# Row maxima that skip NaN: two row pieces for each load, and a separate tile for the 16-bit keys

## The chip, the core and the metric

The kernel runs on one core of a Trainium2 chip. Its engines work in parallel, each through its own queue in order: ScalarE (ACT in the profile), GpSimd (POOL), VectorE (DVE) and SyncE (SP), which here only issues DMA transfers. They wait for each other by semaphores. TensorE (PE) does nothing in this kernel. The on-chip memory has 128 partitions, and a tile is a stretch of bytes in each of them. The metric is the device time of one launch in microseconds (us), the median of several runs.

## What is computed

```python
batch, seq, dim = 32, 2048, 2048
x = np.random.randn(batch, seq, dim).astype(np.float32)
mask = np.random.rand(batch, seq, dim) < 0.1
x[mask] = np.nan
...
np.nanmax(x, axis=-1).astype(np.float32)
```

That is 65,536 rows of 2048 float32 numbers, 537 MB read, and for each row the largest number that is not NaN (a row of NaN alone gives NaN). The output has 65,536 numbers.

## The kernel before

Each partition takes 512 rows. They are cut into groups (`GROUPS`, line 11): twelve groups of 40 rows a partition, each loaded as five tiles `xt` of 8 rows (64 KB a partition, 8.4 MB in all), then a group of 24 rows in tiles of 7, 6, 5, 4 and 2 rows, and one of 8 rows in tiles of 2, 2, 1, 1, 1 and 1: 71 tiles. The pool of `xt` (line 58) has three buffers, so three tiles can be in flight.

Each tile passes four steps, each of which takes the whole tile:

1. SP loads `xt` (line 74). The load waits until VectorE has done with the tile that held the buffer, three tiles ahead.
2. ScalarE (line 77) reads the upper 16 bits of every number as a signed integer, `[:, 1::2]`, so every second 16-bit word, and writes a 16-bit key over them. The activation function (Prelu with a bias and a scale of -1) maps a number's upper half v to 0x7F7F - v; a positive NaN's upper half, 0x7FC0, falls on the function's other slope and gets the key 0x7F7F + 129.
3. GpSimd (line 85) reads the key in the same place and writes 0x7F7F - key over it. Ordinary numbers get their upper half back; NaN gets -129, which makes the number -255 x 2^120, below all the data.
4. VectorE (line 93) takes the maximum of each row of `xt` as float32 into `acc`.

After a group, VectorE makes `none` from `acc` (line 101: which rows hold only NaN) and `fin` from `acc` and `none` (line 110: turns those rows back to NaN). ScalarE's queue issues the store of `fin` (line 113); it stands there ahead of the ScalarE steps of the tiles that follow.

What sets the order is the order in which the code is written, queue by queue, and the buffers of the pools.

Of the kernel before, what the change touches and what calls it, by code (L numbers as in the profile page):

```python
# [1 line left out]

# [4 lines left out]

GROUPS = [(40, [8] * 5)] * 12 + [
    (24, [7, 6, 5, 4, 2]),
    (8, [2, 2, 1, 1, 1, 1]),
]

TOP = 0x7F7F
NAN = 0x7FC0
LOW = -129  # L20

EDGE = TOP + 0.25

NONE = -255.0 * 2.0**120


@with_exitstack
def kernel(
    ctx: ExitStack,
    tc: tile.TileContext,  # L30
    x: bass.AP,
    axis: bass.AP,
    out: bass.AP,
):

    nc = tc.nc
    P = nc.NUM_PARTITIONS
    f32, i32 = mybir.dt.float32, mybir.dt.int32
    i16, u16 = mybir.dt.int16, mybir.dt.uint16
    ALU = mybir.AluOpType

    nd = len(x.shape)
    assert axis in (-1, nd - 1), axis  # L50
    D = x.shape[-1]

    xr = x.bitcast(i32).flatten_outer_dims()
    R = xr.shape[0]
    of = out.bitcast(i32).flatten_outer_dims().rearrange("r c -> (r c)")
    assert R == P * sum(s for s, _ in GROUPS)

    io = ctx.enter_context(tc.tile_pool(name="io", bufs=3))
    res = ctx.enter_context(tc.tile_pool(name="res", bufs=3))
    sing = ctx.enter_context(tc.tile_pool(name="sing", bufs=1))  # L60
    top = sing.tile([P, 1], f32)
    nc.vector.memset(top, EDGE)  # L62

    r0 = 0
    for s, cuts in GROUPS:
        assert sum(cuts) == s
        xg = xr[r0 : r0 + P * s].rearrange("(p s) d -> p s d", p=P)
        og = of[r0 : r0 + P * s].rearrange("(p s) -> p s", p=P)
        r0 += P * s
        acc = res.tile([P, s], f32, tag="acc")  # L70
        at = 0
        for c in cuts:
            xt = io.tile([P, c * D], i32, tag="xt")
            nc.sync.dma_start(
                out=xt, in_=xg[:, at : at + c].rearrange("p c d -> p (c d)")
            )
            nc.scalar.activation(  # L77
                out=xt.bitcast(u16)[:, 1::2],
                in_=xt.bitcast(i16)[:, 1::2],
                func=mybir.ActivationFunctionType.Prelu,  # L80
                bias=top,
                scale=-1.0,
                alpha=float(TOP - LOW) / (EDGE - NAN),
            )
            nc.gpsimd.tensor_scalar(  # L85
                out=xt.bitcast(i16)[:, 1::2],
                in0=xt.bitcast(u16)[:, 1::2],
                scalar1=-1.0,
                scalar2=float(TOP),
                op0=ALU.mult,  # L90
                op1=ALU.add,
            )
            nc.vector.tensor_reduce(  # L93
                out=acc[:, at : at + c],
                in_=xt.bitcast(f32).rearrange("p (c d) -> p c d", c=c),
                axis=mybir.AxisListType.X,
                op=ALU.max,
            )
            at += c
        none = res.tile([P, s], i32, tag="none")  # L100
        nc.vector.tensor_scalar(  # L101
            out=none,
            in0=acc,
            scalar1=NONE,
            scalar2=float(0x00C00000),
            op0=ALU.is_equal,
            op1=ALU.mult,
        )
        fin = res.tile([P, s], i32, tag="fin")
        nc.vector.tensor_tensor(  # L110
            out=fin, in0=acc.bitcast(i32), in1=none, op=ALU.bitwise_or
        )
        nc.scalar.dma_start(out=og, in_=fin)  # L113


# [1 line left out]
_INS = ['x', 'axis']  # L117
_OUTS = [((32, 2048), 'float32')]

_NUMBERS = {'axis': -1}  # L120


# [26 lines left out]
```

## Time and profile before

| | |
|---|---|
| median of 3 runs | 1747.19 us (1747.01 to 1747.41) |
| the profiled execution | 1748.27 us |
| its span, from the first instruction to the last | 1746.5 us |
| VectorE, ScalarE, GpSimd busy | 1143, 1182, 1175 us |
| read from memory, mean rate over the span | 536.87 MB, 308 GB/s |

The profile shows one execution. Busy time counts an engine's instructions; the idle time before an instruction is put down to what released it last. In a row of the timeline stand the start, the length, the engine, the line of the kernel, the operation, its tiles and shapes, the count of merged instructions and the idle time before with its releaser. In a row of the groups stand the line, the engine, the operation, the shapes and the count, then the busy time and the mean length in ns, then the idle time before. In a row of the DMA issues stands the time from issue to landing at the end. The busy share of ScalarE, GpSimd and the DMA engines in 40 slices of the span, in tenths, shows a pattern of peaks and gaps throughout:

```profile
ACT  4865956856857757758668668567577586586553
POOL 0959577587586585595595595595595595595854
DMA  9595976966967867868768669669569669569343
```

### The profile page before, as it was taken

Reading aid. Unit: us, or ns where it says so; the run is one execution under the profiler, and the core shown is the slowest. Engines: PE = TensorE matmul, PEld = TensorE weight load, DVE = VectorE, ACT = ScalarE, POOL = GpSimd, SP = SyncE. Lnnn points to the kernel's source line nnn. Section 1 sums busy time; section 2 is a strip of 40 time slices with the busy share of each in tenths; the row PEclk is TensorE's granted clock in tenths of the full one; section 3 lists DMA queues with packets and bytes.
Section 4 is the critical chain, followed back from the end, with each engine's and each line's share of the span. In section 5 each row is a group of like instructions: output and inputs, shape, how many; then the busy total and the mean of one; then the engine's idle time right before and its main releaser. Section 6 shows DMA issues by size and latency. Waiting matters only on the chain.

```text
span 1746.5 us, 655 instructions
## 1 busy us (share of the span) xinstructions
DVE 1143.4 (65%) x100; ACT 1182.0 (68%) x72; POOL 1174.7 (67%) x75
## 2 busy tenths in 40 slices
DVE  0568585585585585675674774864865856856886
ACT  4865956856857757758668668567577586586553
POOL 0959577587586585595595595595595595595854
DMA  9595976966967867868768669669569669569343
GB/s 420 234 444 246 385 308 269 385 282 294 385 264 312 361 263 338 334 268 360 313 264 384 293 260 408 265 263 429 241 267 410 265 264 428 245 264 411 142 192 144
DMA packets 12244, 537.17 MB, mean 308 GB/s; under 512 B 3152, under 2 KB 3152, under 8 KB 3152
## 3 DMA queue, kind: packets, MB, share of 16 engines
q1 hardware_dynamic: 10224, 536.88, 72.6%
q10 hardware_dynamic: 2016, 0.26, 0.1%
q14 instruction: 4, 0.03, 0.0%
HBM read 536.87 MB, written 0.26 MB: 308 GB/s over the span
## 4 chain that ended last, share of the span: by engine, by line
DVE 26%; POOL 26%; ACT 22%; DMA 19%; issue 6%; ACTq 0%; POOLq 0%; DVEq 0%
POOL xt L85 26%; DVE acc L93 24%; ACT xt L77 22%; DMA xt<-in_x_dram 19%; DVE none L101 2%; ACTq L113 0%; POOLq L144 0%; DVE fin L110 0%; ACTq L77 0%; POOLq L85 0%; DVEq L93 0%
## 5 line engine op out<-in xcount | busy, mean ns | idle before, releaser
L85 POOL TENSOR_SCALAR xt<-xt 128x16384 int16<-128x16384 uint16 (+4 forms) x71 | 1174.5, 16542 | 566.4 <-ACT xt L77 565.6
L77 ACT ACTIVATE xt<-xt,top 128x16384 uint16<-128x16384 int16 (+4 forms) x71 | 1180.7, 16642 | 533.8 <-DMA xt<-in_x_dram 323.1
L93 DVE TENSOR_REDUCE acc<-xt 128x8 f32<-128x16384 f32 (+4 forms) x71 | 1102.6, 15535 | 598.9 <-POOL xt L85 598.9
L101 DVE TENSOR_SCALAR none<-acc 128x40 int32<-128x40 f32 (+2 forms) x14 | 39.1, 2790 | 0.5
L77 ACT ACT_TABLE_LOAD x1 | 1.3, 1283 | 23.0 <-DMA xt<-in_x_dram 23.0
L110 DVE TENSOR_TENSOR fin<-acc,none 128x40 int32<-128x40 int32 (+2 forms) x14 | 2.8, 197 | 0.5
L62 DVE MEMSET top<- 128x1 f32 x1 | 0.1, 59 | 0.8 <-PEq L130 0.8
L130 POOL MEMSET const-float32-0.0<- 128x1 f32 x1 | 0.1, 98 | 0.2 <-issue 0.2
L130 POOL MEMSET const-bfloat16-1.0<- 128x1 bf16 x1 | 0.1, 102 | 0.0
L130 POOL MEMSET const-uint8-127<- 128x1 uint8 x1 | 0.1, 102 | 0.0
L130 POOL MEMSET const-float32-1.0<- 128x1 f32 x1 | 0.1, 98 | 0.0
## 6 DMA issues: line engine op xcount, KB each, us to landing
xt<-in_x_dram SPq DMA_DIRECT2D x1, 7168.0 KB, 19.6
xt<-in_x_dram SPq DMA_DIRECT2D x1, 6144.0 KB, 16.9
xt<-in_x_dram SPq DMA_DIRECT2D x3, 2048.0 KB, 7.3
xt<-in_x_dram SPq DMA_DIRECT2D x1, 5120.0 KB, 14.6
xt<-in_x_dram SPq DMA_DIRECT2D x1, 4096.0 KB, 12.0
xt<-in_x_dram SPq DMA_DIRECT2D x4, 1024.0 KB, 4.7
xt<-in_x_dram SPq DMA_DIRECT2D x60, 22.0
out_dram<-fin ACTq DMA_DIRECT2D x12, 20.0 KB, 19.6
```

The costliest lines, as they stand in the source:

```text
L62: nc.vector.memset(top, EDGE)
L77: nc.scalar.activation(out=xt.bitcast(u16)[:, 1::2], in_=xt.bitcast(i16)[:, 1::2], func=mybir.ActivationFunctionType.Prelu, bias=top, scal ...
L85: nc.gpsimd.tensor_scalar(out=xt.bitcast(i16)[:, 1::2], in0=xt.bitcast(u16)[:, 1::2], scalar1=-1.0, scalar2=float(TOP), op0=ALU.mult, op1= ...
L93: nc.vector.tensor_reduce(out=acc[:, at : at + c], in_=xt.bitcast(f32).rearrange("p (c d) -> p c d", c=c), axis=mybir.AxisListType.X, op=A ...
L101: nc.vector.tensor_scalar(out=none, in0=acc, scalar1=NONE, scalar2=float(0x00C00000), op0=ALU.is_equal, op1=ALU.mult,)
L110: nc.vector.tensor_tensor(out=fin, in0=acc.bitcast(i32), in1=none, op=ALU.bitwise_or)
L130: nc = _bacc.Bacc("TRN2", target_bir_lowering=False, num_devices=1)
```

## The change

- The groups become eleven of 42 rows, one of 28, one of 14 and one of 8. Seventy full tiles have 7 rows (56 KB a partition, `WIDE`), loaded at once; the last 22 rows come in loads of 4 rows down to 1, with up to five loads to a tile.
- ScalarE, GpSimd and VectorE go over a tile in pieces: 4 rows and then 3 in a full tile, 1 to 4 in the last ones. A piece has its own ScalarE, GpSimd and VectorE instruction.
- ScalarE writes the keys of a piece packed into a tile of their own, `kt`, from a new pool `mid` with two buffers of 4 rows (16 KB each). GpSimd reads them there, side by side, and writes the result into every second word of `xt`, as before.
- The store of `fin` goes to SP's queue, behind the first load of the group after the next one; the last two come at the end.
- A small activation on `top` at the start brings the table load of ScalarE ahead of the first load's landing.

```diff
-GROUPS = [(40, [8] * 5)] * 12 + [
-    (24, [7, 6, 5, 4, 2]),
-    (8, [2, 2, 1, 1, 1, 1]),
+FULL = [[4, 3]]
+GROUPS = [[FULL] * 6] * 11 + [
+    [FULL] * 4,
+    [[[4], [3]], [[3], [2], [2]]],
+    [[[2], [1, 1], [1], [1], [1]], [[1]]],
 ]
+WIDE = 7
+PIECE = 4
...
     io = ctx.enter_context(tc.tile_pool(name="io", bufs=3))
+    mid = ctx.enter_context(tc.tile_pool(name="mid", bufs=2))
...
+    warm = sing.tile([P, 1], f32)
+    nc.scalar.activation(out=warm, in_=top, func=PRELU, alpha=0.5)
...
-        for c in cuts:
-            xt = io.tile([P, c * D], i32, tag="xt")
-            nc.sync.dma_start(
-                out=xt, in_=xg[:, at : at + c].rearrange("p c d -> p (c d)")
-            )
-            nc.scalar.activation(
-                out=xt.bitcast(u16)[:, 1::2],
-                in_=xt.bitcast(i16)[:, 1::2],
...
-            nc.gpsimd.tensor_scalar(
-                out=xt.bitcast(i16)[:, 1::2],
-                in0=xt.bitcast(u16)[:, 1::2],
...
+        for tl in g:
+            xt = io.tile([P, WIDE * D], i32, tag="xt")
+            base = at
+            for ld in tl:
+                c = sum(ld)
+                nc.sync.dma_start(
+                    out=xt[:, (at - base) * D : (at - base + c) * D],
+                    in_=xg[:, at * D : (at + c) * D],
+                )
+                if len(stores) > 1:
+                    nc.sync.dma_start(**stores.pop(0))
+                for c in ld:
+                    xp = xt[:, (at - base) * D : (at - base + c) * D]
+                    kt = mid.tile([P, PIECE * D], u16, tag="kt")
+                    nc.scalar.activation(
+                        out=kt[:, : c * D],
+                        in_=xp.bitcast(i16)[:, 1::2],
...
+                    nc.gpsimd.tensor_scalar(
+                        out=xp.bitcast(i16)[:, 1::2],
+                        in0=kt[:, : c * D],
...
+                    nc.vector.tensor_reduce(
+                        out=acc[:, at : at + c],
+                        in_=xp.bitcast(f32).rearrange("p (c d) -> p c d", c=c),
...
-        nc.scalar.dma_start(out=og, in_=fin)
+        stores.append(dict(out=og, in_=fin))
+    for st in stores:
+        nc.sync.dma_start(**st)
```

What stands in the queues, at two places. ScalarE's queue around the end of the first group, before the change (numbered names are the buffers; in brackets what the instruction waits for: DMAHW is a load, Pool is GpSimd):

```order
L77 ACTIVATE xt_82<-xt_82,top_64 128x16384 [waits DMAHW3_49,DVE_49]
L77 ACTIVATE xt_87<-xt_87,top_64 128x16384 [waits DMAHW4_49,DVE_49]
L77 ACTIVATE xt_98<-xt_98,top_64 128x16384 [waits DMAHW5_49,DVE_49]
L113 DMA out_0_dram<-fin_94 128x40 [waits DVE_49]
L77 ACTIVATE xt_103<-xt_103,top_64 128x16384 [waits DMAHW6_49,Pool_49]
```

And ScalarE's queue from its first piece on, after the change:

```order
L96 ACTIVATE kt_74<-xt_72,top_67 128x8192 [waits DMAHW0_49]
L96 ACTIVATE kt_78<-xt_72,top_67 128x6144
L96 ACTIVATE kt_84<-xt_82,top_67 128x8192 [waits DMAHW1_49,Pool_49]
L96 ACTIVATE kt_88<-xt_82,top_67 128x6144 [waits Pool_49]
L96 ACTIVATE kt_94<-xt_92,top_67 128x8192 [waits DMAHW2_49,Pool_49]
```

The store with its wait for VectorE has left this queue; from the third piece on each piece waits for GpSimd, which has to have read the key buffer's last piece.

SP's queue near the end, after the change (`xt_854` is the second tile of the 14-row group, `xt_875` the first of the 8-row group, `fin_839` belongs to the 28-row group):

```order
L87 DMA xt_854<-in_x_dram 128x6144 [waits DMAHW6_49,DVE_49]
L87 DMA xt_854<-in_x_dram 128x4096 [waits DMAHW4_49]
L87 DMA xt_854<-in_x_dram 128x4096
L87 DMA xt_875<-in_x_dram 128x4096 [waits DMAHW7_49,DVE_49]
L92 DMA out_0_dram<-fin_839 128x28 [waits DVE_49]
L87 DMA xt_875<-in_x_dram 128x4096 [waits DMAHW0_49]
L87 DMA xt_875<-in_x_dram 128x2048 [waits DMAHW1_49]
```

The store of the 28-row group stands among the loads of the last tiles and waits for VectorE; the stores ahead of it in this queue (two groups late) have no such wait listed.

More of the change, by code (lines that the diff above doesn't have):

```diff
@@ L47 @@
     ALU = mybir.AluOpType
+    PRELU = mybir.ActivationFunctionType.Prelu
     nd = len(x.shape)
@@ L55 @@
     of = out.bitcast(i32).flatten_outer_dims().rearrange("r c -> (r c)")
-    assert R == P * sum(s for s, _ in GROUPS)
+    rows = [sum(sum(sum(ld) for ld in tl) for tl in g) for g in GROUPS]
+    assert R == P * sum(rows)
     io = ctx.enter_context(tc.tile_pool(name="io", bufs=3))
+    mid = ctx.enter_context(tc.tile_pool(name="mid", bufs=2))
     res = ctx.enter_context(tc.tile_pool(name="res", bufs=3))
@@ L62 @@
     nc.vector.memset(top, EDGE)
+    warm = sing.tile([P, 1], f32)
+    nc.scalar.activation(out=warm, in_=top, func=PRELU, alpha=0.5)
+    stores = []
     r0 = 0
-    for s, cuts in GROUPS:
-        assert sum(cuts) == s
-        xg = xr[r0 : r0 + P * s].rearrange("(p s) d -> p s d", p=P)
+    for s, g in zip(rows, GROUPS):
+        xg = xr[r0 : r0 + P * s].rearrange("(p s) d -> p (s d)", p=P)
         og = of[r0 : r0 + P * s].rearrange("(p s) -> p s", p=P)
@@ L71 @@
         at = 0
-        for c in cuts:
-            xt = io.tile([P, c * D], i32, tag="xt")
-            nc.sync.dma_start(
-                out=xt, in_=xg[:, at : at + c].rearrange("p c d -> p (c d)")
-            )
-            nc.scalar.activation(
-                out=xt.bitcast(u16)[:, 1::2],
-                in_=xt.bitcast(i16)[:, 1::2],
[L80 to L85, printed above, removed]
-                out=xt.bitcast(i16)[:, 1::2],
-                in0=xt.bitcast(u16)[:, 1::2],
[L88 to L99, printed above, removed]
+        for tl in g:
[15 more added lines that the diff above has]
+                        in_=xp.bitcast(i16)[:, 1::2],
+                        func=PRELU,
+                        bias=top,
+                        scale=-1.0,
+                        alpha=float(TOP - LOW) / (EDGE - NAN),
+                    )
+                    nc.gpsimd.tensor_scalar(
+                        out=xp.bitcast(i16)[:, 1::2],
+                        in0=kt[:, : c * D],
+                        scalar1=-1.0,
+                        scalar2=float(TOP),
+                        op0=ALU.mult,
+                        op1=ALU.add,
+                    )
+                    nc.vector.tensor_reduce(
+                        out=acc[:, at : at + c],
+                        in_=xp.bitcast(f32).rearrange("p (c d) -> p c d", c=c),
+                        axis=mybir.AxisListType.X,
+                        op=ALU.max,
+                    )
+                    at += c
```

## The prediction

> **What bounds the kernel now.** I read the page's first part first, to see whether an engine is full, and then the DMA queue.
>
> ```profile
> DVE 1143.4 (65%) x100; ACT 1182.0 (68%) x72; POOL 1174.7 (67%) x75
> q1 hardware_dynamic: 10224, 536.88, 72.6%
> SPq L74 <- DVE acc L93: 1676.5, 67, 55.4
> ```
>
> No engine is full and the loads take 73% of the DMA time. The third line, from the list of what the load queue waited for, names the reason: of 1746.5 us, SP stood 1676.5 us until a VectorE maximum released a buffer. So the bound is the loop load, ScalarE, GpSimd, VectorE, next load through three buffers. The chain of work that ended last (start, length, what) shows its first load and one turn:
>
> ```profile
> 0.74 22.16 DMA xt<-in_x_dram
> ...
> 386.36 18.44 ACT xt L77
> 404.86 18.29 POOL xt L85
> 423.18 17.23 DVE acc L93
> 440.44 2.07 DVE none L101
> 442.53 0.21 DVE fin L110
> 442.76 0.34 ACTq L113
> 443.20 18.43 ACT xt L77
> 461.71 18.30 POOL xt L85
> 480.03 17.23 DVE acc L93
> 497.28 21.80 DMA xt<-in_x_dram
> 519.16 18.43 ACT xt L77
> ```
>
> From 443.20 to 519.16, 76.0 us, three tiles of 8 rows pass. Nothing in a turn overlaps for one tile, since each step takes all 8 rows. From 386.36 to 443.20 the end of a group adds a second loss: ScalarE's queue held the store of the group, which waits for `fin`, ahead of a tile that was ready. Together 132.8 us for 5 tiles, 26.6 each; times 64 tiles' worth of rows, 1700, and a tail.
>
> **Prices.** The groups by line and shape give them (mean ns is the figure before the last bar):
>
> ```profile
> L77 ACT ACTIVATE xt<-xt,top 128x16384 uint16<-128x16384 int16 x60 | 1105.7, 18433 | 474.4 <-DMA xt<-in_x_dram 263.8 <-DVE fin L110 210.6
> L85 POOL TENSOR_SCALAR xt<-xt 128x16384 int16<-128x16384 uint16 x60 | 1099.8, 18331 | 522.5 <-ACT xt L77 522.3
> L93 DVE TENSOR_REDUCE acc<-xt 128x8 f32<-128x16384 f32 x60 | 1033.1, 17218 | 578.1 <-POOL xt L85 578.1
> L77 ACT ACTIVATE xt<-xt,top 128x8192 uint16<-128x8192 int16 x1 | 9.4, 9360 | 13.8 <-DMA xt<-in_x_dram 13.8
> L85 POOL TENSOR_SCALAR xt<-xt 128x8192 int16<-128x8192 uint16 x1 | 9.3, 9257 | 11.6 <-ACT xt L77 11.6
> L93 DVE TENSOR_REDUCE acc<-xt 128x4 f32<-128x8192 f32 x1 | 8.7, 8685 | 7.2 <-POOL xt L85 7.2
> ```
>
> Between the two sizes ScalarE takes (18433 - 9360) / 8192 = 1.1075 ns an element, GpSimd 1.1077 and VectorE 1.0416, each with 0.15 to 0.29 us a piece on top. A 3-row piece (6144 elements) is then 7.09, 6.99 and 6.55 us; a 4-row piece stands in the rows: 9.36, 9.26, 8.69.
>
> For the loads, the page's list of issues, and two neighbouring starts of ScalarE that each ended a wait for a load:
>
> ```profile
> xt<-in_x_dram SPq DMA_DIRECT2D x1, 7168.0 KB, 19.6
> xt<-in_x_dram SPq DMA_DIRECT2D x4, 1024.0 KB, 4.7
> xt<-in_x_dram SPq DMA_DIRECT2D x60, 22.0
> ```
> ```profile
> 119.97 18.39 ACT L77 ACTIVATE xt<-xt,top 128x16384 uint16<-128x16384 int16 x1 [1.31 <-DMA xt<-in_x_dram]
> 139.30 18.42 ACT L77 ACTIVATE xt<-xt,top 128x16384 uint16<-128x16384 int16 x1 [0.94 <-DMA xt<-in_x_dram]
> ```
>
> From issue to landing 7 rows take 4.7 + 6 x (22.0 - 4.7) / 7 = 19.5 us alone (the one row of that size has 19.6). Back to back, 8 rows landed 19.33 us apart, so 7 rows take 16.9: this is the floor of a tile of 7 rows. 512 rows at it are 1237 us.
>
> **The change, part by part.**
>
> 1. *Pieces of 4 and 3 rows.* The buffer is now held for the load, ScalarE's and GpSimd's first piece, and both maxima (GpSimd's second piece runs beside the first maximum). With today's rates: 19.5 + 9.36 + 9.26 + 8.69 + 6.55 + 0.2 (the gaps of 0.02 to 0.08 us in the chain) = 53.6, over three buffers 17.9 us for 7 rows, where now 26.6 go for 8. That step alone removes most of the wait; next late is the load itself (16.9).
>
> 2. *The key tile.* It adds a wait: ScalarE may write a piece only when GpSimd has read the piece two before it. Pieces alternate 4, 3, so one of the two key buffers always holds a 4-row piece, and the 4-row piece of a tile cannot start on ScalarE before GpSimd has ended the 4-row piece of the tile ahead. Behind it in ScalarE's queue stand only further pieces; GpSimd waits for them. This ring costs ScalarE's 4 rows plus GpSimd's 4 rows a tile: 9.36 + 9.26 + 0.14 = 18.8 us at today's rates, which is above both 17.9 and 16.9. So the rates decide.
>
> 3. *The rates of the packed pass* stand in no row. That two engines with different arithmetic take the same 1.108 ns speaks for the access: both read every second 16-bit word and write it back in place. Which of the three costs (the strided read, the strided write, or reading and writing one tile) no row tells. Upper bound: nothing gained, 1.108. Lower: time in proportion to the bytes swept, 4 + 4 an element now, 4 + 2 after, so 0.831 ns, an estimate from these rows; it holds for either engine. A loss isn't excluded, and is priced below. If the strided write costs, ScalarE gains alone (4 rows 7.1); if the strided read, GpSimd alone (4 rows 7.0); if the sharing, both. In each of the three the ring falls to 16.5 or less, and it no longer matters which. I take the gain on ScalarE: 7.1, with GpSimd unchanged.
> The Trainium skill (ScalarE: Activation LUTs, Rules for kernel authors) budgets about 0.3 us an ACTIVATE and 0.83 ns an element. The trace's 1.1075 is a third above that; by that figure a packed 4-row piece would take 7.1 us and the sum would be the same as mine; nothing here rests on it.
>
> 4. *Buffer loop with that rate*: 53.6 - 2.3 = 51.3, a third of it 17.1 us a tile, just above the load's 16.9. ScalarE then is busy 12.5 us of it, GpSimd 16.4, VectorE 15.4.
>
> 5. *Stores on SP, two groups late.* ScalarE no longer waits for `fin`. SP issues the store behind a load, when its `fin` is long done; 12 x 0.34 us of issuing lie inside SP's long waits. Only the 28-row store near the end holds loads behind it: SP waits there for its `fin`, which VectorE reaches after the two maxima of the first tail tile, 8.7 + 6.6 us and the wait for the second piece, about 17. Five loads of 1 and 2 rows stand behind it. In that time GpSimd has 12 rows that were loaded ahead, 27 us: nothing, and up to 10 us if a load was late before. The table load goes under the first load: 1.3 off the start.
>
> ```profile
> L77 ACT ACT_TABLE_LOAD x1 | 1.3, 1283 | 23.0 <-DMA xt<-in_x_dram 23.0
> ```
>
> 6. *The group's two small VectorE steps.* They were off GpSimd's way or caught by it:
>
> ```profile
> 424.14 18.32 POOL L85 TENSOR_SCALAR xt<-xt 128x16384 int16<-128x16384 uint16 x1 [0.99 <-ACT xt L77]
> 440.44 2.06 DVE L101 TENSOR_SCALAR none<-acc 128x40 int32<-128x40 f32 x1
> 442.53 0.20 DVE L110 TENSOR_TENSOR fin<-acc,none 128x40 int32<-128x40 int32 x1
> ...
> 1604.50 48.27 POOL L85 TENSOR_SCALAR xt<-xt 128x16384 int16<-128x16384 uint16 x3 [19.09 <-ACT xt L77]
> 1640.08 12.73 DVE L101 TENSOR_SCALAR none<-acc 128x40 int32<-128x40 f32 x1
> 1743.64 0.17 DVE L101 TENSOR_SCALAR none<-acc 128x8 int32<-128x8 f32 x1
> ```
>
> With GpSimd idle `none` takes 0.17 us (last row); otherwise it ends 0.04 us after GpSimd's instruction does (442.46 and 442.50; 1652.77 and 1652.81). So it is held until GpSimd's instruction ends. After the change GpSimd is in a piece nearly always, and `none` waits up to 9.3 us. But the next maximum waits for that same piece, so only about 0.3 us a group is lost, 3 us in all, if `fin` then runs at once as it does here.
>
> **The sum.** First landing 0.74 + 19.5 = 20.2; third 54.0; 67 more full tiles at 17.1 bring the 70th in at 1200, with the group ends 1203. Its way through ScalarE and GpSimd (7.1 + 9.3 + 7.0 + 0.2) ends at 1227, the first tail piece on GpSimd at 1236. From there VectorE has 22 rows in 12 pieces, 22 x 2.133 + 12 x 0.18 = 49, with one wait of `none` 2.4 at most: 1287. `none`, `fin` and the store (1743.64 to the span's end was 2.9 us) give 1290. The profiled execution took 1748.27 for its span of 1746.5, 1.8 more, and lies 1.1 above the median of 1747.19: **about 1291 us**. If both engines gain, the tile falls to the load's 16.9 and the tail shortens, 1276; if loads land no better than 19.7 us apart (17.2 a tile), 1305.
>
> **Rivals.**
>
> *A. `fin` is caught too (1330 to 1385).* `fin` reads two tiles. Once `none` is through, GpSimd's next piece is ready; the gap between its back-to-back pieces is 0.08 us (61.02 to 61.10 in the chain), and `fin` starts 0.07 us after GpSimd's end (442.46, 442.53). No row shows `fin` beside a starting GpSimd piece. If the piece wins, `fin` is held 7.0 us, the next maximum and its buffer with it, and the load of that buffer is late by as much: 12 x 7.0 = 84, 1375. If GpSimd's 3 rows take 5.3 us, some 1335.
>
> ```profile
> 61.02 0.08 issue
> 61.10 18.33 POOL xt L85
> ```
>
> For: the row of `none` shows the hold is real. Against: the start is a tie, and GpSimd's pieces carry 0.18 us of overhead in which `fin`'s 0.2 us might slip by.
> The Trainium skill (SBUF — State Buffer, Who interferes with whom) says that VectorE and GpSimd share a port pair, that whoever issues first has it for the whole instruction, and that a VectorE instruction with two SBUF inputs contends with a GpSimd one that reads SBUF: by that, this rival's time. The trace agrees for `none`; for `fin` no row decides.
>
> *B. The packed pass gains nothing on either engine (1405; with A, about 1465).* Then the change doesn't do what the packing is for and the ring of part 2 binds: 29.6 (first GpSimd piece, 20.2 + 9.4) + 70 x 18.76 = 1343, then GpSimd's 22 rows, 53, and some 10 for its waits, the last maximum and the store. For: no row shows a packed pass. Against: two engines at one rate.
>
> *C. Slower than before.* The ring decides once it passes 1747 / 73.1 = 23.9 us a tile, that is when a packed write or read costs 0.63 ns an element more than the strided one (2.22 + 0.63 for the two). ScalarE at twice its rate, 18.4 us for 4 rows, would give 70 x 27.8 + 83 = about 2030. Against: it touches fewer bytes than now.
>
> **How the numbers follow.** Forecast (a gain somewhere, `fin` not caught) 0.46; A 0.32; B without A 0.11, with A 0.06; C 0.03; other 0.02. The range takes in the forecast from its lower end, A and B without A: 1272 to 1410, 0.89 by the cases and about 0.8 after errors within them. A measurement of this kernel can tell about 0.2% from no change. Only C is slower, nothing ends near 1747: faster 0.96, same 0.01, slower 0.03.
>
> **What would show it.** Part 1: SP's wait for VectorE shrinks and loads fill over 90% of the DMA time. Part 3: the 8192-element ScalarE row at 7.1 us, GpSimd's at 9.26. Part 2 or B: ScalarE's idle time released by GpSimd, tiles 18.8 us apart. Part 6 or A: `fin` at 0.2 us, or at 5 to 9. I am wrong if a packed row is above 1.11 ns, or if loads run slower in a filled queue than 19.7 us for 8 rows.

## The result and the profile after

| | before | after |
|---|---|---|
| median | 1747.19 us | 1345.3 us (3 runs, 1343.9 to 1346.53) |
| profiled execution, its span | 1748.27, 1746.5 us | 1343.9, 1342.1 us |
| busy: VectorE, ScalarE, GpSimd | 1143, 1182, 1175 us | 1148, 912, 1200 us |

The ratio to the kernel before is 0.7699 (95% interval 0.7682 to 0.7717): faster by 23%. The forecast was 1291 us with a range of 1272 to 1410. The direction and the range held; the point was 54 us short, outside the 1276 to 1305 us that the forecast's own case was given.

The page of the changed kernel: engines, the load queue's share of the DMA time, what the load queue waited for, and the 7-row loads from issue to landing.

```profile
DVE 1147.9 (86%) x181; ACT 912.5 (68%) x154; POOL 1199.8 (89%) x156
q1 hardware_dynamic: 13680, 537.14, 95.4%
SPq L87 <- DVE acc L112: 1224.4, 70, 31.7
xt<-in_x_dram SPq DMA_DIRECT2D x70, 7168.0 KB, 21.7
```

The loads fill 95% of the DMA time instead of 73%. SP still waits for VectorE nearly all the time. The groups by line and shape of the changed kernel:

```profile
L104 POOL TENSOR_SCALAR xt<-kt 128x8192 int16<-128x8192 uint16 x71 | 661.9, 9322 | 119.2 <-ACT kt L96 119.1
L96 ACT ACTIVATE kt<-xt,top 128x8192 uint16<-128x8192 int16 x71 | 505.7, 7122 | 392.8 <-DMA xt<-in_x_dram 388.7 <-POOL xt L104 4.1
L96 ACT ACTIVATE kt<-xt,top 128x4096 uint16<-128x4096 int16 x3 | 11.1, 3709 | 6.2 <-POOL xt L104 6.2
L120 DVE TENSOR_SCALAR none<-acc 128x42 int32<-128x42 f32 x11 | 28.3, 2571 | 0.4
L129 DVE TENSOR_TENSOR fin<-acc,none 128x42 int32<-128x42 int32 x11 | 2.2, 204 | 0.4
L129 DVE TENSOR_TENSOR fin<-acc,none 128x28 int32<-128x28 int32 x1 | 3.3, 3311 | 0.0
```

ScalarE's 4 rows take 7.12 us where they took 9.36, GpSimd's 9.32 as before; `none` takes 2.6 us on the mean (0.17 where nothing holds it), `fin` runs at once (0.20) in all eleven full groups. One turn of a buffer, from the chain that ended last:

```profile
429.29 7.13 ACT kt L96
436.42 0.07 issue
436.49 9.34 POOL xt L104
445.83 0.02 issue
445.86 15.16 DVE acc L112 x2
461.02 0.02 issue
461.03 21.60 DMA xt<-in_x_dram
...
482.72 7.13 ACT kt L96
```

53.4 us for three tiles of 7 rows, 17.8 a tile, against a forecast of 51.3 and 17.1. Every part stands as forecast but the load: 21.6 us, not 19.5.

### The profile page after: what moved, and what is told of

Same layout as the page of the kernel before. It is cut to its first block, busy times and chain, and to the rows that moved or that the text cites. A ratio compares the mean times of both kernels' runs of the same rounds, so it can differ in the third digit from the quotient of the medians.

```text
span 1342.1 us, 945 instructions
## 1 busy us (share of the span) xinstructions
DVE 1147.9 (86%) x181; ACT 912.5 (68%) x154; POOL 1199.8 (89%) x156
## 3 DMA queue, kind: packets, MB, share of 16 engines
q1 hardware_dynamic: 13680, 537.14, 95.4%
## 4 chain that ended last, share of the span: by engine, by line
DMA 38%; DVE 27%; POOL 17%; ACT 13%; issue 4%; another core or an unknown queue 0%; ACTq 0%; SPq 0%; DVEq 0%; POOLq 0%
DMA xt<-in_x_dram 38%; DVE acc L112 26%; POOL xt L104 17%; ACT kt L96 13%; DVE none L120 1%; DVE fin L129 0%; ACTq L96 0%; SPq L87 0%; DVEq L112 0%; POOLq L104 0%
## 5 line engine op out<-in xcount | busy, mean ns | idle before, releaser
L104 POOL TENSOR_SCALAR xt<-kt 128x8192 int16<-128x8192 uint16 (+3 forms) x152 | 1199.6, 7892 | 131.0 <-ACT kt L96 124.5
L112 DVE TENSOR_REDUCE acc<-xt 128x4 f32<-128x8192 f32 (+3 forms) x152 | 1108.2, 7333 | 190.3 <-POOL xt L104 190.3
L96 ACT ACTIVATE kt<-xt,top 128x8192 uint16<-128x8192 int16 (+3 forms) x152 | 911.0, 6037 | 414.7 <-DMA xt<-in_x_dram 397.9
L120 DVE TENSOR_SCALAR none<-acc 128x42 int32<-128x42 f32 (+3 forms) x14 | 35.1, 2508 | 0.4
L129 DVE TENSOR_TENSOR fin<-acc,none 128x42 int32<-128x42 int32 (+3 forms) x14 | 6.2, 440 | 0.4
## 6 DMA issues: line engine op xcount, KB each, us to landing
xt<-in_x_dram SPq DMA_DIRECT2D x70, 7168.0 KB, 21.7
```

The source lines that it names most:

```text
L96: nc.scalar.activation(out=kt[:, : c * D], in_=xp.bitcast(i16)[:, 1::2], func=PRELU, bias=top, scale=-1.0, alpha=float(TOP - LOW) / (EDGE ...
L104: nc.gpsimd.tensor_scalar(out=xp.bitcast(i16)[:, 1::2], in0=kt[:, : c * D], scalar1=-1.0, scalar2=float(TOP), op0=ALU.mult, op1=ALU.add,)
L112: nc.vector.tensor_reduce(out=acc[:, at : at + c], in_=xp.bitcast(f32).rearrange("p (c d) -> p c d", c=c), axis=mybir.AxisListType.X, op=A ...
L120: nc.vector.tensor_scalar(out=none, in0=acc, scalar1=NONE, scalar2=float(0x00C00000), op0=ALU.is_equal, op1=ALU.mult,)
L129: nc.vector.tensor_tensor(out=fin, in0=acc.bitcast(i32), in1=none, op=ALU.bitwise_or)
```

## The experiments

Two theories were open. **Loop**: the tiles come 17.8 us apart because a buffer's turn takes 53.4 us. **DMA**: 56 KB loads, or loads beside busy engines, come no faster.

**e1, the loads alone.** ScalarE's, GpSimd's and most of VectorE's work is left out, and the result with it.

```diff
+        raw = res.tile([P, s], i32, tag="raw")
...
-                    kt = mid.tile([P, PIECE * D], u16, tag="kt")
-                    nc.scalar.activation(
...
-                    nc.gpsimd.tensor_scalar(
...
-                        out=acc[:, at : at + c],
-                        in_=xp.bitcast(f32).rearrange("p (c d) -> p c d", c=c),
+                        out=raw[:, at : at + c],
+                        in_=xp.rearrange("p (c d) -> p c d", c=c)[:, :, 0:8],
```

> ScalarE's and GpSimd's steps are left out, and VectorE's maximum takes 8 of the 2048 numbers of a row into a tile that nobody reads: what is left is the loads with three buffers that come free at once. Theory loop (the changed kernel's tiles are 17.9 us apart because a buffer's turn, load and chain, takes 53.6 us over three buffers; the loads alone could do 16.9): tiles land 16.9 us apart, span about 1245 us. Rival DMA (56 KB loads don't come faster than 17.9 us apart): span about 1310 us.

Measured: 1248.9 us, span 1247.1. Its timeline (VectorE's short maxima follow each landing) and DMA share:

```profile
614.49 0.27 DVE L96 TENSOR_REDUCE raw<-xt 128x4 int32<-128x32 int32 x2 [16.66 <-DMA xt<-in_x_dram]
631.78 0.27 DVE L96 TENSOR_REDUCE raw<-xt 128x4 int32<-128x32 int32 x2 [17.02 <-DMA xt<-in_x_dram]
648.43 0.27 DVE L96 TENSOR_REDUCE raw<-xt 128x4 int32<-128x32 int32 x2 [15.87 <-DMA xt<-in_x_dram]
```
```profile
q1 hardware_dynamic: 13680, 537.14, 99.8%
```

Two tiles in 33.94 us, 17.0 each. The loads can do what the forecast took as their floor. That rules out the size of the loads, not yet the busy engines.

**e4, the keys in place.** Pieces without the key tile.

```diff
-                        out=kt[:, : c * D],
+                        out=xp.bitcast(u16)[:, 1::2],
...
-                        in0=kt[:, : c * D],
+                        in0=xp.bitcast(u16)[:, 1::2],
```

> Pieces of 4 and 3 rows, but the keys written in place in every second word, as before the change; no key tile. Theory loop: ScalarE's 4 rows back at 9.36 us, no key ring, turn 53.6 + 2.2 = 55.8, 18.6 a tile: 1345 + 70 x 0.75 = about 1395 us, so the pieces made most of the gain and the key tile some 50 us. Rival (the packed keys made the gain): well above 1500 us. Rival DMA (17.9 a tile from the loads): 1395 too, but then e1 and e2 stay at 17.9.

Measured: 1386.0 us (one run). ScalarE's 4 rows went back up:

```profile
L94 ACT ACTIVATE xt<-xt,top 128x8192 uint16<-128x8192 int16 x71 | 666.8, 9392 | 158.2 <-DMA xt<-in_x_dram 155.7 <-DVE none L118 2.5
xt<-in_x_dram SPq DMA_DIRECT2D x70, 7168.0 KB, 21.2
```

So of the 402 us gained, the key tile accounts for 1386 - 1345 = 41; the rest came with the pieces, the smaller tiles and the moved stores. It came out 9 us below what loop gave, with loads of 21.2 in place of 21.7.

**e8, GpSimd writing packed.** For its time alone; the write into the rows and so the result is left out.

```diff
-                        out=xp.bitcast(i16)[:, 1::2],
+                        out=kt.bitcast(i16)[:, : c * D],
...
-                        out=acc[:, at : at + c],
-                        in_=xp.bitcast(f32).rearrange("p (c d) -> p c d", c=c),
+                        out=raw[:, at : at + c],
+                        in_=xp.rearrange("p (c d) -> p c d", c=c),
```

> GpSimd writes its result packed over the keys and nothing goes back into the rows; the maximum runs over the raw numbers as int32 into a tile that nobody reads, so the result is left out. For GpSimd's time alone. Theory strided write (writing every second 16-bit word is what costs a third more): 8192 elements in 0.83 to 0.86 ns each, 7.0 to 7.2 us in place of 9.32. Rival (GpSimd's two arithmetic steps set its time): 9.3 us.

```profile
L106 POOL TENSOR_SCALAR kt<-kt 128x8192 int16<-128x8192 uint16 x71 | 498.5, 7021 | 342.8 <-ACT kt L98 342.8
```

The whole kernel took 1259.9 us (one run); GpSimd's 4 rows take 7.02 us, 0.83 ns an element by the slope to 6144 elements (5314 ns). The four cases now separate what one trace could not: a strided read with a packed write is fast (ScalarE after), a packed read with a strided write is slow (GpSimd after), packed both ways is fast even in place (e8), and strided both ways is slow (both engines before). On GpSimd writing every second 16-bit word is what costs a third more. On ScalarE the strided write and the writing in place went together, so that the write is the cause there too is inferred from GpSimd and not shown by itself.

**e2, pieces of 3, 2, 2.**

```diff
-FULL = [[4, 3]]
+FULL = [[3, 2, 2]]
```

> Full tiles in pieces of 3, 2 and 2 rows in place of 4 and 3; all else as in the changed kernel. The way from landing to release becomes about 5.4 + 16.6 + 4.4 + 0.3 = 26.7 us, 5 shorter. Theory loop: the turn falls to 48.4 us, 16.1 a tile, below the loads' 16.9; tiles come 16.9 to 17.1 us apart, 1345 - 70 x 0.85 = about 1287 us. Rival DMA: the loads stay at 17.9, 1345 us. Rival GpSimd (its extra piece, 0.26 us a tile, makes it the bound): 16.6 us of work a tile, so at most as loop says.

Measured: 1311.8 us (ratio to the kernel before 0.7503, interval 0.7491 to 0.7516). Faster as loop has it, but 25 us short. The chain names a new bound, which neither theory had:

```profile
438.74 5.42 ACT kt L96
444.17 0.07 issue
444.24 7.04 POOL xt L104
451.28 0.08 issue
451.36 4.83 POOL xt L104
456.19 0.02 issue
456.21 5.42 ACT kt L96
```

No load stands in it. With three pieces on two key buffers, ScalarE's 3-row piece must wait for GpSimd's first 2-row piece of the tile ahead: 17.47 us a turn of that ring.

**e12, the same with a third key buffer** (the edit is against e2).

```diff
-    [[[4], [3]], [[3], [2], [2]]],
+    [[[2, 2], [3]], [[3], [2], [2]]],
...
-PIECE = 4
+PIECE = 3
...
-    mid = ctx.enter_context(tc.tile_pool(name="mid", bufs=2))
+    mid = ctx.enter_context(tc.tile_pool(name="mid", bufs=3))
```

> Pieces of 3, 2 and 2 rows as in e2, with three key buffers of 3 rows in place of two of 4 (the 4-row load near the end in two pieces of 2). Theory ring (e2's 17.4 us a tile are GpSimd's 3- and 2-row pieces and ScalarE's 3-row piece one after the other, 7.04 + 4.78 + 5.42 + 0.16, since ScalarE must wait for a key buffer; with a third buffer it needn't): bound by the loads, 17.0 us a tile, 1312 - 70 x 0.4 = about 1284 us. Rival (17.4 is GpSimd's own pace beside VectorE, or the loads'): 1312 us.

Measured: 1277.5 us (one run), 34 below e2 and a little under the expectation; ScalarE again waits for loads (318.8 us) and hardly for GpSimd (16.7):

```profile
L96 ACT ACTIVATE kt<-xt,top 128x4096 uint16<-128x4096 int16 (+2 forms) x223 | 924.2, 4204 | 335.5 <-DMA xt<-in_x_dram 318.8 <-POOL xt L104 16.7
```

The ring was the bound of e2, and beside fully busy engines the loads do reach their pace. Rival DMA falls.

**e10, two loads a tile.** Only the load's part of the turn gets shorter.

```diff
-FULL = [[4, 3]]
+FULL = [[4], [3]]
```

> Each full tile is loaded by two transfers, of 4 and of 3 rows, so that ScalarE's first piece can start when 4 rows are in; pieces and chain as in the changed kernel. Only the load's part of the turn gets shorter, by 3 rows at 2.4 us, 7.2 us: 46.4 us a turn, 15.5 a tile, below the loads' 16.9. Theory loop: bound by the loads, 1345 - 70 x 0.85 = about 1286 us. Rival (a load's fixed time, 4.7 - 2.4 = 2.3 us, is paid twice in the queue): 1345 us or above.

Measured: 1277.0 us, ratio 0.7304 (0.7292 to 0.7315). The load queue's packets fill 98.2% of the DMA time:

```profile
q1 hardware_dynamic: 23760, 537.14, 98.2%
```

The chain of work in the changed kernel was left as it was and 68 us went with the load's part: the term that the forecast had wrong is the one that the kernel was bound by. The 9 us below the expectation lie in the tail: from ScalarE's start on the last full tile to VectorE's end 83 us pass here (1189.3 to 1272.4), 91 in the changed kernel. From 20 to 1170 us of the span e10, e12 and e3 move 431, 433 and 433 GB/s, as e1 does (433); the changed kernel moves 413.

**e3, five rows and four buffers.**

```diff
-FULL = [[4, 3]]
+FULL = [[3, 2]]
...
-WIDE = 7
-PIECE = 4
+WIDE = 5
+PIECE = 3
...
-    io = ctx.enter_context(tc.tile_pool(name="io", bufs=3))
-    mid = ctx.enter_context(tc.tile_pool(name="mid", bufs=2))
+    io = ctx.enter_context(tc.tile_pool(name="io", bufs=4))
+    mid = ctx.enter_context(tc.tile_pool(name="mid", bufs=3))
...
-                if len(stores) > 1:
+                if len(stores) > 2:
```

> Tiles of 5 rows in pieces of 3 and 2, four buffers of 40 KB, three key buffers, stores three groups late. A turn is about 14.6 + 2.2 (load) + 5.4 + 7.1 + 6.5 + 4.4 + 0.3 = 40.5 us over four buffers, 10.1 a tile, against 12.1 for the load and 12.0 for GpSimd. Theory loop: bound by the loads, 512 / 5 x 12.1 = 1240, with head and tail 1275 to 1285 us. Rival DMA (2.55 us a row whatever the loop): about 1340 us.

Measured: 1279.8 us, ratio 0.732 (0.7309 to 0.7331), as loop said. e3, e10 and e12 come to within 3 us of each other by three different ways. All three beat both kernels, and stand some 30 us above e1's loads alone.

**e9, pieces of 3, then 4.**

```diff
-FULL = [[4, 3]]
+FULL = [[3, 4]]
```

> Full tiles in pieces of 3 and then 4 rows; all else as in the changed kernel, the loads and the key ring (16.6 us) too. From landing to release: 5.40 + 7.06 + 9.33 + 8.69 + 0.25 = 30.7 us where 4 and 3 have 7.12 + 9.33 + 8.69 + 6.54 + 0.2 = 31.9. Theory loop (a microsecond less in a buffer's turn is a third of one a tile): 70 x 1.2 / 3 = 28 us less, about 1317 us. Rival (the loads' own straggling in a queue that runs dry sets 17.9 a tile, whatever the chain): 1345 us.

Measured: 1343.2 us (1342.0 to 1344.6): the total says that loop is wrong. The profile says otherwise. Inside a group the turn did get shorter, 52.7 us from 482.72 to 535.38, with a load no shorter than before (21.87):

```profile
482.72 5.42 ACT kt L96
...
513.42 21.87 DMA xt<-in_x_dram
...
535.38 5.42 ACT kt L96
```

What was won there was lost at the ends of groups, where the small VectorE steps now often come while GpSimd is at the beginning of a 4-row piece. VectorE's timeline:

```profile
138.26 8.23 DVE L120 TENSOR_SCALAR none<-acc 128x42 int32<-128x42 f32 x1
246.45 0.65 DVE L120 TENSOR_SCALAR none<-acc 128x42 int32<-128x42 f32 x1
351.96 0.19 DVE L120 TENSOR_SCALAR none<-acc 128x42 int32<-128x42 f32 x1
352.18 9.14 DVE L129 TENSOR_TENSOR fin<-acc,none 128x42 int32<-128x42 int32 x1
```

From one `none` to the next, the group that begins with a hold of 8.23 us takes 108.2 us (138.26 to 246.45), the next, without one, 105.5 (246.45 to 351.96), which is 17.6 a tile; at 352.18 it is `fin` that is held, for 9.14. Six of the eleven full groups end with such a hold. The group behind a hold takes 108.5 us on the mean, the others 105.2, so a hold costs 3.3 us; six are 20 us, about what the shorter turns had won (106.8 us a group in the changed kernel). So the expectation failed by a second effect and not by the loop; e9 alone would not have settled it, e10 does.

**e6, `fin` a step later.** A small maximum that copies `none` stands between the two.

```diff
+        gap = res.tile([P, s], i32, tag="gap")
+        nc.vector.tensor_reduce(
+            out=gap,
+            in_=none.rearrange("p (s o) -> p s o", o=1),
+            axis=mybir.AxisListType.X,
+            op=ALU.max,
+        )
...
-            out=fin, in0=acc.bitcast(i32), in1=none, op=ALU.bitwise_or
+            out=fin, in0=acc.bitcast(i32), in1=gap, op=ALU.bitwise_or
```

> The changed kernel with one more small VectorE step between none and fin (a maximum over one element each, a copy; it takes about 0.2 us), so that fin starts some 0.2 us later than now. Theory tie (fin starts 0.07 us after GpSimd's piece ends and gets through just ahead of the next piece, which starts at 0.08): now the next piece is first, fin is held 7.1 us in each of the 11 full groups, 1345 + 11 x 7 = about 1420 us, and its mean rises from 0.2 to about 7 us. Rival (fin isn't held by GpSimd at all): 0.2 us each, about 1348 us.

Measured: 1381.7 us (one run). VectorE at the end of the fourth group:

```profile
470.06 2.78 DVE L120 TENSOR_SCALAR none<-acc 128x42 int32<-128x42 f32 x1
472.88 0.20 DVE L129 TENSOR_REDUCE gap<-none 128x42 int32<-128x42 int32 x1
473.11 6.79 DVE L136 TENSOR_TENSOR fin<-acc,gap 128x42 int32<-128x42 int32 x1
479.83 45.24 DVE L112 TENSOR_REDUCE acc<-xt 128x4 f32<-128x8192 f32 x6
```

`gap`, a maximum over one tile, ran in 0.20 us beside GpSimd's next piece, which began with it at 472.9; `fin`, which reads two tiles, came 0.2 us later and was held 6.8 us, here and on the mean of the eleven full groups (6800 ns). A quarter of a microsecond decides. Reading one tile is not enough to get by, though: `none`, which reads only `acc`, is held too. The price was half of what was expected: 36 us for 11 holds, 3.3 each, as in e9. Part of the rest is made up by VectorE itself: behind the hold it goes over three tiles without a wait (the last row, 45.24 us), where otherwise it waits some 1.8 us for GpSimd ahead of a tile (at 437.96 and 454.88). Whether that is all of it was not tried.

**e7, the kernel before with its stores on SP.**

```diff
+            if len(stores) > 1:
+                nc.sync.dma_start(**stores.pop(0))
...
-        nc.scalar.dma_start(out=og, in_=fin)
+        stores.append(dict(out=og, in_=fin))
+    for st in stores:
+        nc.sync.dma_start(**st)
```

> The kernel before, with the stores on the load queue, two groups late, alone. Theory: a turn at a group's end loses its store wait, 132.8 us for 5 tiles become 5 x 25.3 = 126.6, 12 x 6.2 = 75 off: about 1672 us. Rival (the buffers' turn sets it whatever ScalarE waits for): 1747 us.

Measured: 1671.9 us (one run). The reading of the old chain, 76.0 us a turn and a store that cost 6.2 us a group, is borne out: some 75 us could have been had from the kernel before by moving the stores. That it is met within a microsecond is luck; the kernel before itself took 1751.25 us in its run beside this one, 4 more than in the result.

**e5, the changed kernel with its stores on ScalarE.**

```diff
-                if len(stores) > 1:
-                    nc.sync.dma_start(**stores.pop(0))
...
-        stores.append(dict(out=og, in_=fin))
-    for st in stores:
-        nc.sync.dma_start(**st)
+        nc.scalar.dma_start(out=og, in_=fin)
```

> The changed kernel with the stores back on ScalarE's queue at the end of each group. ScalarE then waits for fin before the next tile's first piece: fin comes about 32 + 2.5 us after the last tile of a group landed, the next tile lands 17.9 us after it, so about 16 us are lost in each of 12 groups: about 1345 + 190 = 1535 us. Rival (the wait hides in ScalarE's idle time, a third of the span): under 1370 us.

Measured: 1344.6 us (one run): no loss at all, the theory missed. The timeline shows why:

```profile
462.24 0.20 DVE L127 TENSOR_TENSOR fin<-acc,none 128x42 int32<-128x42 int32 x1
462.47 0.34 ACTq L130 DMA_DIRECT2D out_dram<-fin  x1
464.81 12.43 ACT L94 ACTIVATE kt<-xt,top 128x8192 uint16<-128x8192 int16 x2 [6.75 <-DMA xt<-in_x_dram]
```

The store stands in the queue behind the first tile of the next group, not at the group's end as the expectation had it, and ScalarE then waits for a load until 464.8 anyway; `fin` is there at 462.4. (In the kernel before, too, the store stands behind one tile of the next group, `xt_98` in the listing of the queue, and ahead of the second.) With pieces the way from ScalarE to `fin` is short enough to hide. Moving the stores was worth 75 us to the kernel before and nothing to this one.

**e11, the last stores later.**

```diff
-                if len(stores) > 1:
+                if len(stores) > 2:
```

> The stores go three groups late, so that the 28-row group's store no longer holds the last five loads, which stood behind it for 25 us. Theory hidden (VectorE is busy without a break from 1296 us to the end and sets the tail): within 1 us of 1345. Rival (those loads and GpSimd's idle 5.4 us before its last pieces set the tail): 1338 to 1340 us.

Measured: 1342.8 us, but from 1339.3 to 1346.4, too wide for the question. The profiles answer it better: from GpSimd's first instruction on the last full tile to the end of the span 86.4 us (1255.71 to 1342.1) in the changed kernel, 85.9 (1258.66 to 1344.6) here, although the 5.4 us that GpSimd idled ahead of its last pieces are gone. The held loads cost nothing that can be seen.

## Why the prediction was right, and where it was short

- *Bound before: a buffer's turn.* Right; e7's one run has the time that this reading gives.
- *Part 1, pieces.* Right in form. With the changed kernel's 42-row groups and SP stores, e4 shows that pieces without the key tile reach 1386 us; its loads took 21.2 us, where the sum had 19.5.
- *Parts 2 and 3, ring and rates.* Right, and the choice of ScalarE as the engine that gains was right too (7.12 against 7.1 forecast). e8 gives the reason on GpSimd, which the prediction had left open: the strided write; for ScalarE it is the likely one. Rival B, no gain, falls: 7122 ns against 9360. The Trainium skill's 0.83 ns an element for ScalarE (ScalarE: Activation LUTs, Rules for kernel authors) agrees with the rows of packed writes: (7122 - 3709) / 4096 = 0.833. With the strided write the rows have 1.108.
- *Part 4, the buffer loop: the step that failed, by a size.* The form was right (turn over three buffers, just above the loads' own 16.9), but the load in it was taken as 19.5 us, that of a load on its own. It measured 21.7 on the median. A third of 2.2 us is 0.73 a tile, times 67 is 49 us. The trace agrees: ScalarE began the last full tile at 1248.5 where the forecast had it land at 1203, 45 us late (the forecast had 3 us for the group ends); the tail has most of the rest. The loads themselves can do 17.0 (e1), and e10 and e12, which by their expectations take 7 and 5 us out of the turn, get down to the loads' pace. A long load does no harm by itself: in e12 the 7-row loads take 22.9 us, but there the turn has slack. What makes a load in this kernel longer is seen at the handover. After the release at 461.02 the DMA engines run on for a moment with the load ahead, then move hardly anything:

```profile
461.00:463.00 2.00, 1.93 (x4) 0.00 (x0) 1.92 (x2) 1.00 1.30 459
463.00:465.00 2.00, 2.00 (x2) 0.00 (x0) 2.00 (x1) 1.00 0.24 86
465.00:467.00 2.00, 2.00 (x1) 1.76 (x1) 2.00 (x1) 1.00 0.94 401
```

(windows of 2 us of the changed kernel; the last two columns are the DMA share and GB/s; shares above 1 show how coarse so short a window is). In e1, where two more loads always wait, no such hole stands in the same windows. This handover is a strong case: at the one near 406 us the emptiest window has a share of 0.65, and from 20 to 1170 us the share is 0.98, against 1.00 in e1, some 23 us idle. Besides, the packets took 95.4% of 1342.1 = 1280 us of the 16 engines, against 99.8% of 1247.1 = 1245 in e1 for the same bytes. In e12, with ScalarE and GpSimd at least as busy but the loads queued, it is 97.6% of 1275.2 = 1245 again. So of the lost time the smaller part is idle and the larger is slower packets; why they are slower in a queue that runs dry was not tried.
- *Part 5, stores.* The costs were nothing, as said (e5, e11). But the gain that the prediction saw in freeing ScalarE from `fin` exists only in the kernel before (e7); with pieces there was nothing to free.
- *Part 6 and Rival A.* `fin` won the tie in all eleven full groups (0.20 us), so A did not happen, though the measured time lies inside the stretch that A was given. Its mechanism is real: e6 holds `fin` 6.8 us by a quarter of a microsecond, e9 once by chance, and the tail of the changed kernel has one of 3.3 us. The rule of the Trainium skill (SBUF — State Buffer, Who interferes with whom) that a VectorE instruction with two SBUF inputs contends with a GpSimd one that reads SBUF, which no row had shown for `fin`, agrees with these holds. So does its other half, that one with at most one SBUF input, outside the 2-port modes, does not contend: `gap` was not held. The prediction put `none` under the two-input rule, but `none` reads only `acc`. It is caught all the same (2.6 us on the mean, up to 8.9 in e9) and `gap` is not; what makes the difference no run here separates. The price, 7 us a group, was twice what e6 measured.
- *The tail.* The forecast let some 85 us pass from the landing of the last full tile to VectorE's end; it took 91 (ScalarE began that tile at 1248.5, VectorE ended at 1339.8), with `none` and `fin` of the 28-row group taking 5.6 and 3.3 us.

## What to carry to other kernels

When a ring of buffers is bound just above the pace of its loads, take the load's time from loads that meet others in the queue, not from one alone, or give the ring enough slack (shorter last pieces, split loads, another buffer) that it doesn't matter: here three such ways each gave some 67 us more. Draw every ring, the small ones too: two key buffers that fit two pieces a tile became the bound with three. And ask what a small two-input VectorE step would wait for if it started a moment later.

## What the runs showed of the hardware

- Reading and writing every second 16-bit word in place takes 1.108 ns an element on ScalarE and on GpSimd; writing packed takes 0.833 ns. On GpSimd the strided read costs nothing: 9257 ns for 8192 elements read strided, 9322 read packed, both written strided. ScalarE reads strided in every run; with a packed write 8192 elements take it 7122 ns.
- `fin`, a VectorE step that reads two tiles, is held to the end of a GpSimd piece that began just before (6.8 of 7.03 us, e6). `none`, which reads one, is held too (up to 8.9 us, e9). The maxima, which also read one tile, are not: 0.20 us for `gap`, and 8.69 us for 4 rows while GpSimd is busy 89% of the time.
- Three loads in flight kept the DMA engines at 99.8% (e1); with each load issued as the one ahead ends, the same bytes took 3% more of the engines' time (1280 us against 1245).
